# Second mixer: the values of groups 1 and 2 from x itself in fp32, with the norm's weights in the moving operand

## The chip, the cores and the metric

The kernel runs on one core of a Trainium2 chip. The metric is device time in microseconds (us) of one execution, as the median over several runs. TensorE's clock is granted at one of two levels, 1.2 or 2.4 GHz; the profile gives it as a share, 0.5 or 1.0.

## The reference, cut to what matters

A decoder trunk of two layers over 512 tokens, model width 1024. The change is in the second layer's mixer. Each token row of x is normalized, multiplied by a weight per model column, and projected:

```python
def rms_norm(x, g):
    y = x * rsqrt(mean(x * x, axis=-1) + EPS)
    return y * g

proj = rms_norm(x, norm_mix) @ w_in          # 512 x 1024 @ 1024 x 2560
# three groups of four heads, each with q, k, v of 256 columns; (window, dilation):
DIL_PATTERNS = ((128, 1), (512, 4), (2048, 16))
# each query attends to itself and to t-d, t-2d, ... back to t-window
```

The root of a token's mean square is one factor per token, so it may be multiplied in after the projection. The weight g belongs to a model column, which is the dimension that the projection sums over, so it may go to either operand of the product.

## The kernel before, in words

x lies in SBUF transposed (`xT`, 8 blocks of 128 model columns x 512 tokens, fp32). A plain fp32 product is avoided: `prep(3)` makes two tensors from xT times g, `xh` (rounded to the type fp32r) and `xl` (the rest), and each weight tile is split by `wsplit` into `wh` and `wl` in the same way. A product is then the three fp32r matmuls xh wh, xl wh and xh wl.

`layer1` is woven from two generators. `products` issues the projections: two tiles for the memory heads' queries, four tiles of queries and keys of group 0, the values of group 0, tiles 6 to 9 of the groups 1 and 2 (first pair of heads), the values of group 1, tiles 10 to 13 (second pair of heads), the values of group 2, then the output projection's memory half. `attention` issues memory attention, scores, transposes and the products with the values. `_weave` takes their steps in turn. The order on TensorE is as written; on the other engines and the DMA queue a planner orders the instructions by a simulated time line.

`values(g)` computes the values of group g with tokens on the partitions: the stationary operand is a block of 128 tokens of xh or xl, the moving one 256 columns of the weights (line 403 to 405 in `token_major`). Group 0 takes neighbouring tokens. Groups 1 and 2 take tokens by their residue modulo 4, so every fourth column is read (`by_residue`). Per group there are 4 blocks of tokens and 8 blocks of model columns. Line 1010 multiplies the result by the factor per token on ScalarE and puts it into `v`.

Weights are loaded on SP's DMA queue into `wf`, a ring of two buffers of one megabyte (`load`, line 168; a load waits until the buffer's last reader is done). `wh` and `wl` are rings of three. `token_weights(..., True)` splits the value weights in two halves: the first with cast and subtraction on VectorE (lines 50, 51), the second with the cast on ScalarE (line 48) and the subtraction on GpSimd. Loads of the second layer go through the two buffers in this order: seven of the input projection (two tiles each) with the three of the values among them, one for each half of the output projection, then those of the feed-forward network.

The strided stationary operand and full fp32 matmuls both occur elsewhere: `ssq_cols` (line 256) sums squares per token with a moving operand of 2 columns of ones, once with neighbouring tokens and once by residue, and the final norm (line 1185) multiplies 128x256 in fp32.

Of the kernel before, what the change touches and what calls it, by code (L numbers as in the profile page):

```python
# [12 lines left out]
AF = mybir.ActivationFunctionType  # L13
ALU = mybir.AluOpType
# [3 lines left out]
KT = D // 128  # L18
# [46 lines left out]
class _Trunk:  # L65
# [328 lines left out]
            wl += [l[:, k * n:(k + 1) * n] for k in range(4)]  # L394
        return wh, wl

    def token_major(self, out, w, ks, xh, xl, i, by_residue=False):

        wh, wl = w
        mm = self.nc.tensor.matmul  # L400
        b = slice(i, None, 4) if by_residue else slice(i * 128, (i + 1) * 128)
        for k in ks:
            mm(out, xh[k][:, b], wh[k], start=k == 0, stop=False)
            mm(out, xl[k][:, b], wh[k], start=False, stop=False)
            mm(out, xh[k][:, b], wl[k], start=False, stop=k == KT - 1)
# [531 lines left out]
    def layer1(self):  # L937
        nc, mm = self.nc, self.nc.tensor.matmul
        xh, xl, parts = self.prep(3)
        ws = self.chunks("in1", list(range(14)), lo=("gpsimd", "vector"), hi=(None, None))  # L940
        pq = []
        for j in range(2):
            p = self.psum_any()
# [41 lines left out]
        def g12_scores(pr, r, QK):  # L985
# [6 lines left out]
            for s in range(2):  # L992
                if r + s == 0:
# [2 lines left out]
                                P[1, pr][:, s * 1024 + r * 256:s * 1024 + (r + 1) * 256],  # L996
                                st12[pr][:, r, s:s + 1], st12[pr][:, r, 2 + s:3 + s])

        def values(g):
            w = self.token_weights(self.io["v1"][g], 256, True)  # L1000
            for r in range(4):
                p = self.psum("acc")[:, :256]
                for k in range(0, KT, 4):
                    self.token_major(p, w, range(k, k + 4), xh, xl, r, by_residue=g > 0)
                    if k == 0:
                        yield
                if r == 0:
                    V[g] = self.big("v", F32)
                c = cols if g == 0 else self.cols4
                self.values(p, c[:, r:r + 1], V[g][:, r * 256:(r + 1) * 256])  # L1010
                yield
# [56 lines left out]
        def products():  # L1068
# [3 lines left out]
            done.add("qk0")  # L1072
            yield from qk(0, qk0[1])
            yield from values(0)
            done.add("qk1")
            done.add("v0")
# [3 lines left out]
            for n, _ in enumerate(values(1)):  # L1080
                if n == 4:
                    done.add("qk2")
                yield
# [5 lines left out]
            for n, _ in enumerate(values(2)):  # L1089
                if n == 0:  # L1090
                    mem_out = [(o, self.inverse(den)) for o, den in self.mem_out]
                if n == 4:
                    done.add("qk3")
                if n == 4:
                    mem_out = [self.finish_pair(*a) for a in mem_out]
                yield
# [241 lines left out]
```

## Time and profile before

| | before |
|---|---|
| median of 3 runs | 1280.42 us (1276.65 to 1281.71) |
| profiled execution | 1287.35 us, span 1285.6 us |
| mean granted clock | 0.973 |
| TensorE matmul | 1218.7 us (95% of the span) |
| TensorE weight load | 983.7 us (77%) |
| VectorE | 586.0 us (46%) |
| ScalarE | 498.7 us (39%) |
| GpSimd | 389.4 us (30%) |
| DMA | 109.98 MB, 86 GB/s |

The engines are PE (TensorE's matmuls), PEld (its weight loads, which overlap them), DVE (VectorE), ACT (ScalarE), POOL (GpSimd) and SP (the queue that issues the loads). Matmuls are pipelined: the durations shown contain the drain and overlap, so the pace of a sequence is read from the starts. Times are from the start of the span.

### The profile page before, as it was taken

What the parts mean: (1) busy time and instruction counts of PE and PEld (TensorE: products, weight loads), DVE (VectorE), ACT (ScalarE), POOL (GpSimd) and SP (SyncE); (2) the same over time, 40 slices, a digit from 0 to 9 for tenths busy, and PEclk for the clock granted to TensorE, in tenths of its full rate; (3) what the DMA queues carried; (4) which work ended last, traced back from release to release, by engine and by line L of the source; (5) the groups of instructions that cost most, each with busy time, mean ns of one, the idle gap of its engine ahead of it and who ended that gap; (6) DMA issues with size and microseconds to landing.
All of it is one profiled execution on the core that took longest, in us unless ns stands there. A gap on an engine that the chain in (4) does not pass through costs nothing.

```text
span 1285.6 us, 14958 instructions
## 1 busy us (share of the span) xinstructions
PE 1218.7 (95%) x5868; PEld 983.7 (77%) x5868; DVE 586.0 (46%) x1054; ACT 498.7 (39%) x859; POOL 389.4 (30%) x242
## 2 busy tenths in 40 slices
PE   6688979999999999999998999999999999999997
PEld 5467657677888888888886779887788888888886
DVE  7789976548333333322224542548533333331212
ACT  6564666525323322322223764534332233222222
POOL 4637464244222122212222322333322221121222
PEclk9789999999999999999998999989899999999998
DMA  5402132212222222222233111211222222222221
GB/s 179 131 33 101 49 113 72 70 36 97 78 88 97 98 99 98 78 90 90 90 111 107 66 66 34 97 35 41 92 98 89 80 94 98 99 90 90 91 90 66
DMA packets 30214, 109.98 MB, mean 86 GB/s; under 512 B 2495, under 2 KB 12095, under 8 KB 21695
## 3 DMA queue, kind: packets, MB, share of 16 engines
q1 hardware_dynamic: 29598, 108.50, 24.1%
q8 instruction: 46, 0.75, 0.2%
q10 hardware_dynamic: 544, 0.52, 0.1%
q14 instruction: 26, 0.20, 0.0%
HBM read 105.74 MB, written 3.28 MB: 85 GB/s over the span
## 4 chain that ended last, share of the span: by engine, by line
PE 81%; DVE 12%; DMA 3%; issue 1%; ACT 1%; POOL 1%; SPq 0%; DVEq 0%; ACTq 0%; POOLq 0%
PE psS L226 5%; PE psS L225 5%; PE psS L227 5%; PE psT L225 3%; PE psT L227 3%; PE psT L226 3%; PE psacc L225 3%; PE psacc L226 3%; PE psacc L227 3%; PE psacc L200 3%; PE psS L414 3%; PE psS L200 3%; PE psS L202 3%; PE psS L201 3%; PE psacc L202 3%; PE psacc L201 3%
## 5 line engine op out<-in xcount | busy, mean ns | idle before, releaser
L51 POOL TENSOR_TENSOR wl<-wf,wh 128x1024 fp32r<-128x1024 f32 x98 | 238.5, 2434 | 684.6 <-ACT wh L48 621.8
L48 ACT CAST wh<-wf 128x1024 fp32r<-128x1024 f32 (+1 forms) x178 | 183.6, 1032 | 527.9 <-issue 171.3
L51 DVE TENSOR_TENSOR wl<-wf,wh 128x1024 fp32r<-128x1024 f32 (+1 forms) x95 | 118.5, 1247 | 94.1 <-ACT wh L48 94.1
L225 PE MATMUL psS<-xh,wh 128*128 128x512 f32 x296 | 120.0, 405 | 6.8 <-ACT wh L48 6.8
L227 PE MATMUL psS<-xh,wl 128*128 128x512 f32 x296 | 119.2, 403 | 2.8 <-DVE wl L51 2.8
L226 PE MATMUL psS<-xl,wh 128*128 128x512 f32 x296 | 118.9, 402 | 2.8 <-DVE xl L310 2.8
L225 PE MATMUL psT<-xh,wh 128*128 128x512 f32 x200 | 81.1, 405 | 0.0
L227 PE MATMUL psT<-xh,wl 128*128 128x512 f32 x200 | 80.7, 403 | 0.0
L226 PE MATMUL psT<-xl,wh 128*128 128x512 f32 x200 | 80.7, 403 | 0.0
L225 PE MATMUL psacc<-xh,wh 128*128 128x512 f32 x192 | 77.3, 403 | 0.0
L226 PE MATMUL psacc<-xl,wh 128*128 128x512 f32 x192 | 76.9, 401 | 0.0
L227 PE MATMUL psacc<-xh,wl 128*128 128x512 f32 x192 | 76.9, 400 | 0.0
L225 PEld LDWEIGHTS psS<-xh,wh 128*128 128x128 f32 x296 | 56.8, 192 | 20.5 <-ACT wh L48 6.8
L227 PEld LDWEIGHTS psS<-xh,wl 128*128 128x128 f32 x296 | 56.7, 191 | 17.2 <-DVE wl L51 4.2
L226 PEld LDWEIGHTS psS<-xl,wh 128*128 128x128 f32 x296 | 56.8, 192 | 16.7 <-DVE xl L310 3.3
L294 POOL TENSOR_TENSOR ssq<-ssq,t 128x512 f32<-128x512 f32 (+1 forms) x34 | 50.8, 1493 | 55.1 <-ACT t L284 53.9
L213 PE MATMUL psacc<-xh,wh 128*128 128x512 f32 x144 | 62.9, 437 | 0.0
L652 DVE TENSOR_TENSOR raw<-psacc,R 128x512 f32<-128x512 f32 x22 | 15.2, 691 | 103.1 <-PE psacc L227 103.1
L215 PE MATMUL psacc<-xh,wl 128*128 128x512 f32 x144 | 58.1, 404 | 0.0
L214 PE MATMUL psacc<-xl,wh 128*128 128x512 f32 x144 | 58.0, 403 | 0.0
L339 POOL TENSOR_TENSOR raw<-raw,table 128x512 f32<-128x512 f32 x21 | 26.9, 1283 | 72.7 <-ACT raw L336 54.9
L627 DVE TENSOR_TENSOR xT<-xT,psacc 128x512 f32<-128x512 f32 x44 | 30.1, 686 | 38.7 <-PE psacc L202 38.6
(335 smaller groups left out, 2812.7 us busy)
## 6 DMA issues: line engine op xcount, KB each, us to landing
wf<-in_gu SPq DMA_DIRECT2D x44, 1024.0 KB
wf<-in_dn SPq DMA_DIRECT2D x16, 1024.0 KB
wf<-in_in SPq DMA_DIRECT2D x13, 1024.0 KB
wf<-in_dn SPq DMA_DIRECT2D x16, 384.0 KB
wf<-in_v SPq DMA_DIRECT2D x3, 1024.0 KB
xT<-in_x SPq DMA_DIRECT2D x8, 256.0 KB
wf<-in_mk SPq DMA_DIRECT2D x2, 1024.0 KB
wf<-in_mv SPq DMA_DIRECT2D x2, 1024.0 KB
```

Of the source, the lines that this page charges most:

```text
L48: nc.scalar.copy(hi, src)
L51: lo_engine.tensor_tensor(out=lo, in0=src, in1=hi.bitcast(F32), op=ALU.subtract)
L200: mm(out, wh[k], xh[k], start=first and k == 0, stop=False)
L201: mm(out, wh[k], xl[k], start=False, stop=False)
L202: mm(out, wl[k], xh[k], start=False, stop=last and k == n - 1)
L213: mm(out, wh[:, s], xh[k], start=k == 0, stop=False)
L214: mm(out, wh[:, s], xl[k], start=False, stop=False)
L215: mm(out, wl[:, s], xh[k], start=False, stop=k == KT - 1)
L225: mm(out, wh[:, s], xh[k], start=k == 0, stop=False)
L226: mm(out, wh[:, s], xl[k], start=False, stop=False)
L227: mm(out, wl[:, s], xh[k], start=False, stop=k == KT - 1)
L294: engine.tensor_tensor(out=parts[part], in0=parts[part], in1=sq, op=ALU.add)
```

## The change

The values of groups 1 and 2 no longer use xh, xl, wh and wl. The weights are loaded, and each of their 8 blocks of 256 columns is multiplied in place by g (odd blocks on VectorE, even ones on ScalarE). The matmul then takes xT itself, every fourth column, as stationary operand and the scaled weights as moving operand, both fp32: one matmul in the code per block in place of three. Group 0 keeps its form, and `token_major` loses its flag. Steps of the weave stay where they were.

```diff
--- before.py
+++ after.py
@@ -394,11 +394,11 @@
             wl += [l[:, k * n:(k + 1) * n] for k in range(4)]
         return wh, wl
 
-    def token_major(self, out, w, ks, xh, xl, i, by_residue=False):
+    def token_major(self, out, w, ks, xh, xl, i):
 
         wh, wl = w
         mm = self.nc.tensor.matmul
-        b = slice(i, None, 4) if by_residue else slice(i * 128, (i + 1) * 128)
+        b = slice(i * 128, (i + 1) * 128)
         for k in ks:
             mm(out, xh[k][:, b], wh[k], start=k == 0, stop=False)
             mm(out, xl[k][:, b], wh[k], start=False, stop=False)
@@ -996,12 +996,27 @@
                                 P[1, pr][:, s * 1024 + r * 256:s * 1024 + (r + 1) * 256],
                                 st12[pr][:, r, s:s + 1], st12[pr][:, r, 2 + s:3 + s])
 
+        def scaled_weights(g):
+
+            w = self.load(self.io["v1"][g], [KT * 256])
+            for k in range(KT):
+                b = w[:, k * 256:(k + 1) * 256]
+                if k % 2:
+                    nc.vector.tensor_scalar(b, b, self.gains[:, 3, k:k + 1], None, op0=ALU.mult)
+                else:
+                    nc.scalar.activation(b, b, AF.Copy, scale=self.gains[:, 3, k:k + 1])
+            return w
+
         def values(g):
-            w = self.token_weights(self.io["v1"][g], 256, True)
+            w = scaled_weights(g) if g else self.token_weights(self.io["v1"][g], 256, True)
             for r in range(4):
                 p = self.psum("acc")[:, :256]
                 for k in range(0, KT, 4):
-                    self.token_major(p, w, range(k, k + 4), xh, xl, r, by_residue=g > 0)
+                    if g:
+                        for a in range(k, k + 4):
+                            mm(p, self.xT[:, a, r::4], w[:, a * 256:(a + 1) * 256], start=a == 0, stop=a == KT - 1)
+                    else:
+                        self.token_major(p, w, range(k, k + 4), xh, xl, r)
                     if k == 0:
                         yield
                 if r == 0:
```

## Rows read from the trace of the kernel before

**Rows 1.** The page: busy time of the engines, and the chain that ended last.
```profile
PE 1218.7 (95%) x5868; PEld 983.7 (77%) x5868; DVE 586.0 (46%) x1054; ACT 498.7 (39%) x859; POOL 389.4 (30%) x242
...
PE 81%; DVE 12%; DMA 3%; issue 1%; ACT 1%; POOL 1%; SPq 0%; DVEq 0%; ACTq 0%; POOLq 0%
```

**Rows 2.** Stretches: us; PE, PEld, DVE, ACT, POOL busy; PEclk, DMA share, GB/s.
```profile
779.40:808.20 28.80, 28.80 (x166) 27.29 (x164) 6.39 (x17) 10.67 (x21) 3.65 (x2) 1.00 0.05 13
833.00:862.90 29.90, 28.46 (x154) 27.16 (x153) 12.58 (x24) 11.76 (x26) 8.94 (x7) 0.89 0.12 37
851.20:858.00 6.80, 6.80 (x35) 6.46 (x34) 2.30 (x8) 2.84 (x10) 0.00 (x0) 0.50 0.00 0
```

**Rows 3.** Timeline of PE in group 1's values: start us, duration us, what.
```profile
787.61 0.40 PE L404 MATMUL psacc<-wh,xl 128*128 128x256 f32 x1
...
795.61 0.40 PE L405 MATMUL psacc<-wl,xh 128*128 128x256 f32 x1
```

**Rows 4.** Timeline of PE in group 0's values, neighbouring tokens.
```profile
729.38 0.28 PE L404 MATMUL psacc<-wh,xl 128*128 128x256 f32 x1
...
731.88 0.28 PE L405 MATMUL psacc<-wl,xh 128*128 128x256 f32 x1
```

**Rows 5.** Timeline of PE's weight loads, neighbouring tokens, then by residue.
```profile
680.99 1.10 PEld L256 LDWEIGHTS psacc<-ones,ssq 128*128 128x128 f32 x8
...
688.71 1.50 PEld L256 LDWEIGHTS psacc<-ones,ssq 128*128 128x128 f32 x6
```

**Rows 6.** Line 256, these loads: ns min/median/max, first and last start us.
```profile
L256 PEld LDWEIGHTS psacc<-ones,ssq x8: 188/192/193, 681.0 to 681.9; 128*128 128x128 f32 x8
...
L256 PEld LDWEIGHTS psacc<-ones,ssq x6: 329/329/329, 688.7 to 689.9; 128*128 128x128 f32 x6
```

**Rows 7.** Timeline of PE in the final norm, full fp32.
```profile
1269.31 0.59 PE L1185 MATMUL psacc<-raw,ones 128*128 128x256 f32 x2
```

**Rows 8.** Line 1185: ns min/median/max, first and last start us.
```profile
L1185 PE MATMUL psacc<-raw,ones x4: 377/430/519, 1269.3 to 1277.8; 128*128 128x256 f32 x4
```

**Rows 9.** Timeline of PE, products of 512 columns, neighbouring stationary columns.
```profile
684.20 0.39 PE L225 MATMUL psS<-xh,wh 128*128 128x512 f32 x1
...
686.48 0.39 PE L226 MATMUL psS<-xl,wh 128*128 128x512 f32 x1
```

**Rows 10.** The tile wf: ns min/median/max of its casts, subtractions, scalings.
```profile
L48 ACT CAST wh<-wf x178: 833/1052/1077, 5.7 to 1257.7; 128x1024 fp32r<-128x1024 f32 x162, 128x768 fp32r<-128x768 f32 x16
L51 POOL TENSOR_TENSOR wl<-wf,wh x98: 2348/2403/4253, 21.1 to 1254.8; 128x1024 fp32r<-128x1024 f32 x98
...
L483 DVE TENSOR_SCALAR mh<-wf,gains x4: 343/344/1176, 181.7 to 183.3; 128x256 fp32r<-128x256 f32 x4
L485 ACT ACTIVATE mh<-wf,gains x4: 499/506/522, 181.8 to 183.0; 128x256 fp32r<-128x256 f32 x4
```

**Rows 11.** Timeline of SP's queue: loads of tiles 12, 13 and out1b.
```profile
774.34 0.37 SPq L176 DMA_DIRECT2D wf<-in_in  x1
...
831.30 0.37 SPq L176 DMA_DIRECT2D wf<-in_out1b  x1
```

**Rows 12.** Stretches, the DMA behind the load of 774.34.
```profile
775.30:778.80 3.50, 3.50 (x24) 2.30 (x24) 1.77 (x2) 1.72 (x2) 0.26 (x1) 1.00 0.89 300
```

**Rows 13.** Timeline of PE, the first product of tile 12.
```profile
822.00 0.39 PE L213 MATMUL psacc<-xh,wh 128*128 128x512 f32 x1
```

**Rows 14.** Timeline of PE and ACT in group 2; [idle before <-releaser].
```profile
847.52 0.59 ACT L443 COPY frow<-psT 128x512 f32<-128x512 f32 x1 [2.76 <-PE psT L427]
...
849.17 0.33 PE L414 MATMUL psS<-qkh 64*128 64x128 f32 x2 [0.77 <-ACT qkh L48]
...
850.29 0.33 PE L414 MATMUL psS<-qkl,qkh 64*128 64x128 f32 x2 [0.68 <-DVE qkl L51]
```

**Rows 15.** Timeline of PE in group 2's values, at half clock.
```profile
855.78 0.44 PE L405 MATMUL psacc<-wl,xh 128*128 128x256 f32 x1
...
857.88 0.37 PE L405 MATMUL psacc<-wl,xh 128*128 128x256 f32 x1
```

## The prediction

> **What bounds the kernel now.** I read the page first: TensorE is busy 95% of the span and carries 81% of the chain of waits, so a change in its work counts unless something else is late where it is made [rows 1]. Then the table of stretches, cut at the two places that the change touches. The values of group 1 lie in 779.4 to 808.2 us, those of group 2 in 833.0 to 862.9 [rows 2]. In the first stretch TensorE is busy all of its 28.80 us at full clock, VectorE 6.39, ScalarE 10.67, GpSimd 3.65: nothing beside it is near its limit. In the second it is busy 28.46 of 29.90, and 6.8 us of it run at half clock. So the time of these products is what the stage costs, almost one for one.
>
> What a product costs is read from starts in the timeline, since the listed durations contain the drain and overlap. In group 1, 34 products of 256 columns start between 787.61 and 795.61: 8.00/34 = 0.2353 us each [rows 3]. Group 0 does the same three products per block with a stationary block of neighbouring columns: 22 starts from 729.38 to 731.88, 0.1136 us each [rows 4]. The moving operand is the same width, so the doubled time belongs to the load of a stationary block taken at every fourth column.
>
> The row sums show that the load alone does it. The small products that sum squares (2 columns, fp32) show loads back to back with nothing to stream: 8 neighbouring ones take 1.10 us, and with 0.19 for the last, (1.10-0.19)/7 = 0.13 each; 6 strided ones take 1.50, one of them 0.329 long, (1.50-0.33)/5 = 0.234 each [rows 5, 6]. That is the 0.2353 of group 1 to within 1%.
>
> **The change part by part.** *The products.* Each of groups 1 and 2 has 4 residues x 8 blocks x 3 = 96 products now. They take 96 x 0.2353 = 22.6 us. Afterwards there are 4 x 8 = 32 matmuls in full fp32. The trace shows how such a matmul runs: the small sums are 4 matmuls in the code and 8 loads and 8 products in the trace, so each is two load-and-product pairs [rows 5, 6]. Hence 64 pairs per group, each with a strided load. What the load of a strided fp32 block costs is in the same rows: 0.234. What two passes over 256 fp32 columns cost is in the final norm: a matmul of 128x256 whose two products span 0.59 us, one being 0.377 long, so 0.59-0.377 = 0.21 from start to start [rows 7, 8].
>
> Not shown is a strided fp32 load together with a 256-column fp32 product. From below, the pair can't be shorter than its load, 0.234; from above, load and product one after the other are 0.234+0.21 = 0.446. I take 0.236, next to the lower end, for two reasons: the strided load with a 256-column single pass costs 0.2353, hardly more than the load alone, so that product lies beneath the load; and 512-column products with their loads start every (686.48-684.20)/10 = 0.228 us, where load and columns in turn would be 0.13 plus at least 0.21 [rows 9]. Then a group takes 64 x 0.236 = 15.1 us in place of 22.6, and the two groups save 2 x 7.5 = **15.0 us**. With 0.25 for the pair it would be 2 x (22.6-16.0) = 13.2. The break-even lies at 22.6/64 = 0.353.
>
> The Trainium skill speaks against this in "TensorE: Matmul & The Clock Gate", "Part 3: Packing small matmuls — row/col tiling": a weight load overlaps with a running matmul only when the row groups differ, which full 128-row blocks never do. By that rule the sum is the 0.446 and the change is a loss (first rival); the 0.228 and the 0.2353 above disagree with it. The same page's "LDWEIGHTS (loading the stationary operand)" prices a load by its columns alone, 128/1.2 = 107 ns; an estimate from it, with no dearer load for strides, puts the old form at group 0's 96 x 0.1136 = 10.9 us and the new one at 64 x 0.21 = 13.4, a loss of 2.5 per group. The strided rows at 0.234 disagree with it and decide.
>
> *Preparing the weights.* Removed per group: a cast and a subtraction on VectorE, a cast of 1.05 us on ScalarE, a subtraction of 2.40 on GpSimd. Added: 4 scalings of 128x256 on ScalarE at 0.51 (2.0 us) and 4 on VectorE at 0.34 (1.4) [rows 10]. TensorE waits for them only if they come late. Group 1's weights were cast and freed by 774.34, when the next load took their buffer [rows 11], 5 us before they are used; the scalings need less time and don't wait for buffers of the split halves. I count nothing. If the cover were gone, 2.0 us per group would show.
>
> *The buffer held longer.* The weights now are the moving operand, so one of the two load buffers is held until the group's last product. The load of tiles 12 and 13 of the input projection, issued at 774.34, then waits until group 1 ends, by 808.2-7.5 = 800.7. On the SP queue group 2's weights, then the output projection's, stand behind it. A megabyte lands 4.5 us after its issue: the DMA is busy until 778.8 for the load of 774.34 [rows 11, 12]. So tiles 12 and 13 are in at 805.2; cast and subtraction add 1.05+2.40, 808.7. TensorE starts on tile 12 at 822.0 now [rows 13], 814.5 then: 5.8 us to spare. Group 2's weights land behind them, about 809.7 if the two share the queues, and are wanted at 833.0-7.5 = 825.5. The second output projection's load waits for group 2's end, about 862.9-15.0 = 848, where it went at 831.3; its product comes after the attention's last join, so I count nothing there. If the 5.8 were used up, TensorE would wait in front of tile 12 for what is missing.
>
> *Split buffers set free.* Tiles 10 to 13 no longer queue for the three split buffers behind the values. That takes work off the moment when the values end; TensorE was not waiting for it, so nothing.
>
> *The wait in group 2.* TensorE stands at 849.17 and 850.29 for 0.77+0.68 us, because the last query/key cast sits on ScalarE behind a copy that waits for TensorE's own transposes; the clock falls behind it [rows 2, 14]. After the change TensorE arrives there 40 x 0.236 = 9.4 us after tile 13, not 14. If the cast goes ahead of the copy the wait goes, up to 1.5 us gained; if the order stays, so does the wait, and the clock matters more. At half clock the old products still start every (857.88-855.78)/9 = 0.233 us [rows 15], since the load sets their pace; the new ones would need twice 0.21 = 0.42 there. A stretch of 6.8 us would pass 16 of them, not 29: 13 x 0.236 = 3.1 us lost. From -3.1 to +1.5, I take 0.
>
> **The sum.** The profiled execution took 1287.35 us, 1285.6 of it span and 1.75 around it; minus 15.0 it would be 1272.3. It lies 6.9 above the median of the runs, 1280.42. The saving is TensorE's own time in two stretches at full clock for the most part, so I take it off the median: **1265.4 us**.
>
> **The rivals.**
> 1. *Load and product in turn.* Place: the 128 pairs of the two groups; price 0.446 each, so 2 x (28.5-22.6) = 11.8 us more, 1292. It decides from 0.353 per pair on. For it: no row has this pair. Against: [rows 3, 9].
> 2. *New waits and half clock eat it.* Shorter values cover less of ScalarE's and VectorE's chain (their order is planned anew), and each wait brings a half-clock stretch that now costs. One such wait as at 849 in each group: 2 x (1.5+3.1) = 9.2 lost, 1280.4-15.0+9.2 = 1274.6. For it: the wait at 849 exists. Against: the first stretch has none, with ScalarE busy 10.7 of 28.8. A late tile 12 belongs here.
> 3. *Another engine sets the end.* If the attention's chain through ScalarE and VectorE needed the whole stretch anyway, nothing is gained: 1280. Against: their busy time [rows 2].
>
> **How the numbers follow.** The forecast 0.78, its own range 1262 to 1270 (a pair at 0.25 and some wait above; the wait at 849 gone below). Rival 2 0.12, rival 1 0.06, rival 3 0.04. A measurement of this kernel can tell some 0.5% from no change, 6.4 us: faster means below 1274.0. The forecast and over half of rival 2 lie there: 0.86. Same, with the rest of rival 2 and rival 3: 0.08. Slower: 0.06. Range 1261 to 1275: it takes in the pair's cost up to 0.28 and most of rival 2, and leaves out the serial end.
>
> **What the profile after would show.** 64 products per group starting every 0.236 us, the loads 0.33 long; the stretch of group 1 about 21.3 us, that of group 2 about 22.4. The load of tiles 12 and 13 issued as group 1 ends and no idle time of TensorE ahead of tile 12. The wait in group 2 gone or as before. The prediction is wrong if the pairs start more than 0.30 us apart, if TensorE idles over 5 us more between 779 and the feed-forward, or if the products fall into a half-clock stretch for over 10 us.

## The result and the profile after

The changed kernel takes 1266.37 us (median of four runs) where the kernel before, beside it on the same chip, takes 1280.45: a ratio of 0.9882 [0.9844, 0.992]. One of the four runs was slow, 2760 us; the ratio leaves it out, and the median of the other three is 1265.67. Three more timings gave 0.9916 [0.9887, 0.9944], 0.9901 [0.9874, 0.9927] and 0.9885 [0.9854, 0.9916]. The forecast was 1265.4. The profiled execution took 1261.48 us, 1259.8 of it span.

Two lines of the page of the changed kernel: busy time, share of the span and instructions of the engines, the answer to [rows 1].

```profile
PE 1191.5 (95%) x5804; PEld 963.8 (77%) x5804; DVE 585.3 (46%) x1058; ACT 499.7 (40%) x865; POOL 385.7 (31%) x240
...
PE 78%; DVE 13%; DMA 3%; ACT 2%; POOL 2%; issue 2%; SPq 0%; DVEq 0%; POOLq 0%; ACTq 0%
```

TensorE has 64 products fewer (192 became 128) and 27.2 us less busy time, nearly twice what the change is worth by the timings. So the page alone does not answer how large the gain is. The stretches of the values of groups 1 and 2 do (columns as in [rows 2]):

```profile
773.00:794.80 21.80, 21.80 (x135) 19.70 (x132) 5.20 (x16) 10.27 (x24) 3.62 (x2) 1.00 0.00 1
819.50:842.40 22.90, 20.54 (x122) 19.03 (x121) 10.58 (x23) 12.65 (x27) 6.06 (x5) 1.00 0.14 47
```

Group 1 went from 28.80 us to 21.80, group 2 from 29.90 to 22.90. Group 2 now holds 2.36 us in which TensorE is idle, and no half clock. From the first product of group 1 to the first of the output projection that follows both groups, the changed kernel shows these starts in TensorE's timeline:

```profile
773.06 2.13 PE L1017 MATMUL psacc<-wf,xT 128*128 128x256 f32 x8
...
842.31 0.49 PE L200 MATMUL psacc<-oh,wh 128*128 128x512 f32 x1
```

That is 69.25 us. The same two starts of the kernel before lie at 779.44 and 862.84, 83.40 apart. **The stage is 14.15 us shorter.** Added up from each product's start to the next instruction's start: group 1's products 23.62 to 16.44 (-7.2), group 2's 23.08 to 16.20 (-6.9); the old wait of [rows 14] is gone (-1.45); a new one came (+2.36); attention scores that had run at half clock run at full (-0.65). Together -13.8, which leaves 0.3 to small things.

The two spans differ by 25.8 us, not 14. About 9.4 of the rest lie in the feed-forward stages, which no edit touches: the two stretches of the code from the first feed-forward to layer 1, and from the last one's start to the end, took 368.97 and 362.49 us in the profile before and 364.34 and 357.71 in this one (counted from the product of line 268 in each, the first to that of layer 1, the second to the end of the last product). Two rows, first before, then after, of the same length of time within the first feed-forward:

```profile
320.00:520.00 200.00, 200.00 (x859) 162.01 (x858) 69.05 (x91) 59.71 (x74) 43.25 (x18) 1.00 0.25 90
```
```profile
320.00:520.00 200.00, 200.00 (x875) 163.97 (x874) 70.96 (x94) 61.78 (x77) 43.30 (x18) 1.00 0.26 95
```

TensorE is never idle and the granted clock is 1.00 in both, yet one runs 859 products and the other 875: products of 512 columns start 0.2333 us apart in one execution and 0.2289 in another. Either pace comes in either stage, whatever the edit: the repeated profile of the changed kernel has 368.97 in the first and 357.7 in the last, the run below with fp32 and neighbouring columns has the slower pace in the last alone, and edited forms of the kernel before have the faster one in both. So a comparison of two profiles is made here on the stage that was changed, and of kernels on the timings.

### The profile page after: what moved, and what is told of

The parts are those of the page before. It is cut to its first block, busy times and chain, and to the rows that moved or that the text cites. A ratio compares the mean times of both kernels' runs of the same rounds, so it can differ in the third digit from the quotient of the medians.

```text
span 1259.8 us, 14831 instructions
## 1 busy us (share of the span) xinstructions
PE 1191.5 (95%) x5804; PEld 963.8 (77%) x5804; DVE 585.3 (46%) x1058; ACT 499.7 (40%) x865; POOL 385.7 (31%) x240
## 4 chain that ended last, share of the span: by engine, by line
PE 78%; DVE 13%; DMA 3%; ACT 2%; POOL 2%; issue 2%; SPq 0%; DVEq 0%; POOLq 0%; ACTq 0%
PE psS L227 5%; PE psS L226 5%; PE psS L225 5%; PE psT L226 3%; PE psT L227 3%; PE psT L225 3%; PE psacc L227 3%; PE psacc L226 3%; PE psacc L225 3%; PE psacc L200 3%; PE psS L200 3%; PE psS L202 3%; PE psS L201 3%; PE psS L414 3%; PE psacc L202 3%; PE psacc L201 3%
## 5 line engine op out<-in xcount | busy, mean ns | idle before, releaser
L51 POOL TENSOR_TENSOR wl<-wf,wh 128x1024 fp32r<-128x1024 f32 x96 | 233.7, 2436 | 636.3 <-ACT wh L48 594.0
L48 ACT CAST wh<-wf 128x1024 fp32r<-128x1024 f32 x176 | 181.2, 1031 | 512.8 <-issue 164.2
```

Source lines behind the costliest of these rows:

```text
L48: nc.scalar.copy(hi, src)
L51: lo_engine.tensor_tensor(out=lo, in0=src, in1=hi.bitcast(F32), op=ALU.subtract)
```

## The experiments

Theory L: the pace of a pair is set by the load of a block taken at every fourth column, and the gain is the number of such loads. Theory P: the gain comes from the work that left the other engines (casts, split buffers). Theory W: waits and the clock decide, not the products. The times of stages below are differences of starts in the timelines. In all of them the ratio is to the kernel before on the same chip.

**The changed kernel again.** No edit.

> The changed kernel once more, beside the next three. Theory L (the strided load sets the pace: 64 loads at 0.233 us per group in place of 96): the pairs start 0.233 apart, the stretch of group 1's values takes 21.8 us, that of group 2 22.9 with a wait of 2.4 us in it, and the run 1265 to 1268. Theory P (the gain comes from the splits that are gone and the buffers they freed, not from TensorE) and theory W (it comes from the wait and the half-clock stretch in group 2 that are gone) expect the same of this run.

1266.44 us, 0.9916 [0.9887, 0.9944]; the stage is 69.27, the new wait is there. The later two, with no edit either:

> The changed kernel once more, beside the three above: 1264 to 1268, with the wait of 2.4 us in group 2.

> The changed kernel beside it: 1264 to 1268, one wait of 2.4 us in group 2.

1265.81 and 1261.84 us; the last lies below the 1264 to 1268 expected.

**Three passes, neighbouring columns** (the kernel before, edited):

```
-        b = slice(i, None, 4) if by_residue else slice(i * 128, (i + 1) * 128)
+        b = slice(i * 128, (i + 1) * 128)
```

> The kernel before, with groups 1 and 2 reading neighbouring tokens as stationary operand (the values stand in other places, so the output is another). Theory L: the products start 0.114 us apart, not 0.235; 96 x 0.114 = 10.9 us per group in place of 22.6, 23 us less in all, from which waits for the query/key chain take back up to 3.5 per group: 1257 to 1264. Theories P and W: the splits, the buffers and the order of the other engines are those of before, so 1280 (P), or no less than 1278 (W).

1258.34 us, 0.9861 [0.9831, 0.9891]. One of the three passes, by its loads (ns, minimum/median/maximum):

```profile
L403 PEld LDWEIGHTS psacc<-wh,xh x64: 186/188/330, 774.1 to 837.1; 128*128 128x128 f32 x64
```

The products start 0.114 to 0.118 apart, and group 1 takes 12.1 us instead of 23.6, with all casts and splits in place. That is the price of the stride by itself: 11.5 us of products in a group, more than the 7.2 of the change. P and W cannot give this.

**Full fp32, neighbouring columns** (the changed kernel, edited):

```
-  mm(p, self.xT[:, a, r::4], w[:, a * 256:(a + 1) * 256], start=a == 0, stop=a == KT - 1)
+  mm(p, self.xT[:, a, r * 128:(r + 1) * 128], w[:, a * 256:(a + 1) * 256], start=a == 0, stop=a == KT - 1)
```

> The changed kernel, with neighbouring tokens in place of every fourth (another output). Theory L: the load falls to 0.13 and the columns set the pace, 0.213 to 0.215 per pair, 64 x 0.215 = 13.8 in place of 15.0: 1.2 us less per group, 1263 to 1265, and the stretch of group 1 20.6. If the fp32 products themselves set the 0.233, the pace stays and so does the time, 1266. Should load and product still add up partly, the pace falls by more than 0.02.

1263.37 us, 0.989 [0.9858, 0.9923]. Its timeline in group 1, and the loads of both groups:

```profile
781.64 4.70 PE L1017 MATMUL psacc<-wf,xT 128*128 128x256 f32 x21
```
```profile
L1017 PEld LDWEIGHTS psacc<-wf,xT x128: 186/190/337, 775.2 to 841.9; 128*128 128x128 f32 x128
```

With 0.379 for the last, (4.70-0.379)/20 = 0.216 per pair. With a cheap load the two passes over 256 fp32 columns set the pace; with a strided one, at 0.233, the load does. The columns of the changed kernel lie almost wholly beneath its loads. In this run a half-clock stretch fell on the values of group 2, the granted clock being the seventh figure of the stretch's row:

```profile
826.90:830.30 3.40, 3.40 (x10) 2.68 (x9) 0.69 (x1) 0.00 (x0) 2.66 (x2) 0.50 0.00 0
```

Pairs start 0.427 apart there, twice 0.21, while the loads beneath them have time to spare.

**Two passes of three, strided** (the kernel before, the xl product left out in groups 1 and 2):

```
-            mm(out, xl[k][:, b], wh[k], start=False, stop=False)
+            if not by_residue:
+                mm(out, xl[k][:, b], wh[k], start=False, stop=False)
```

> The kernel before, with the product of the low part of x left out in groups 1 and 2: 64 fp32r products per group, each with a strided load, splits and buffers as before. Theory L: 64 loads at 0.234 = 15.0 us per group whatever the columns (one pass here, two in the changed kernel), so the same stretch of 21.8 to 22 us for group 1 as the changed kernel, and 1265 to 1268. Theory P: nothing of the preparation is saved, 1280. Theory W: as the wait in group 2 falls, 1276 to 1280.

1266.32 us, 0.9929 [0.9898, 0.996]. 64 strided loads as in the changed kernel, but one-pass products, splits and old buffers. Its loads:

```profile
L403 PEld LDWEIGHTS psacc<-wh,xh x64: 307/330/335, 772.3 to 841.7; 128*128 128x128 f32 x64
```

The products start 0.235 apart and group 1 takes 16.12 us, against 16.44 in the changed kernel. The number of strided loads decides, whether one pass or two are streamed over them. Two parts of group 2's stretch ran at half clock in this run:

```profile
824.10:827.50 3.40, 3.40 (x16) 3.40 (x16) 0.69 (x1) 0.00 (x0) 2.03 (x3) 0.50 0.00 0
834.30:842.50 8.20, 8.20 (x46) 7.29 (x45) 3.31 (x12) 3.66 (x12) 2.36 (x1) 0.50 0.01 2
```

Its products kept starting 0.233 apart there, and the group took 17.53 us including a wait of 1.5: load-bound products hardly feel the clock, as [rows 15] had shown.

**The splits kept** (the changed kernel, with an unread split of each half of the weights, cast and subtraction, ahead of the scaling):

```
+            for c in range(2):
+                self.wsplit(w[:, c * 1024:(c + 1) * 1024], (nc.vector, nc.gpsimd)[c], (nc.vector, None)[c])
```

> The changed kernel, which also does the old casts and subtractions of the value weights of groups 1 and 2 ahead of the scaling, into halves that nothing reads. Theory L (the gain is the 64 strided loads in place of 96): TensorE's stretches stay as in the changed kernel, 21.8 and some 23 us, and the run 1264 to 1269. Theory P (the gain is the splits that are gone): back to 1275 to 1280.

1262.52 us, 0.9873 [0.9847, 0.9898]. Its stretches of the two groups:

```profile
773.80:795.60 21.80, 21.80 (x134) 19.69 (x132) 9.14 (x18) 12.14 (x26) 3.69 (x3) 1.00 0.12 48
822.50:844.30 21.80, 21.77 (x121) 19.96 (x121) 11.77 (x24) 12.54 (x28) 8.73 (x6) 0.92 0.14 49
```

VectorE is busy 9.14 us instead of 5.20 in group 1's stretch, ScalarE 12.14 instead of 10.27, and TensorE's time stays 21.80. The stage is 70.35 us (69.25 without the splits); the 1.1 lie in group 2, part of which ran at half clock here (0.92), and the run came out a little below the 1264 expected. P's casts and subtractions fall: work taken from engines that were not late is worth nothing here. No product holds the split halves in this run; that holding them is not the price either is shown by the run of two passes, which holds them and gains as much in group 1.

**Every second column** (the kernel before, blocks of tokens at a stride of 2):

```
-        b = slice(i, None, 4) if by_residue else slice(i * 128, (i + 1) * 128)
+        b = slice(i // 2 * 256 + i % 2, i // 2 * 256 + 256, 2) if by_residue else slice(i * 128, (i + 1) * 128)
```

> The kernel before (three passes), with every second token of 256 in groups 1 and 2 as stationary operand, not every fourth (another output). A stride of four fp32 is 16 bytes, two are 8. If only a stride of 16 bytes or more is dear, the products start some 0.114 to 0.13 us apart and the run is that of neighbouring tokens, 1257 to 1262. If any stride is, they stay 0.235 apart and the run 1278 to 1282. If the price goes with the bytes skipped, it lies between, near 0.17, and the run near 1268. The Trainium skill (SBUF — State Buffer, the part on cachelines) has lines of 16 bytes with full bandwidth for at least two hits per line; that speaks for the first.

1261.05 us, 0.9864 [0.9835, 0.9893]. Its loads, and two starts of its products in group 1, 20 products apart:

```profile
L403 PEld LDWEIGHTS psacc<-wh,xh x64: 193/195/331, 772.7 to 839.4; 128*128 128x128 f32 x64
```
```profile
779.72 0.28 PE L403 MATMUL psacc<-wh,xh 128*128 128x256 f32 x1
...
782.12 0.28 PE L405 MATMUL psacc<-wl,xh 128*128 128x256 f32 x1
```

2.40/20 = 0.120. A stride of two fp32 columns (8 bytes) costs 0.120 against 0.114 for neighbours; a stride of four (16 bytes) costs 0.235. The price is not linear in the stride: it lies between these two.

**Where the new wait comes from.** In group 2 of the changed kernel the second block of values waits. Its timeline of TensorE, VectorE and ScalarE (in brackets the idle time before, and what ended it):

```profile
819.51 3.88 PE L1017 MATMUL psacc<-wf,xT 128*128 128x256 f32 x16
...
822.20 1.14 ACT L48 CAST qkh<-raw 128x512 fp32r<-128x512 f32 x1 [1.76 <-DVE raw L340]
823.36 2.34 ACT L336 COPY raw<-psacc 32x512 f32<-32x512 f32 x4
825.75 3.64 PE L1017 MATMUL psacc<-wf,xT 128*128 128x256 f32 x14 [2.36 <-ACT raw L336]
```

The accumulators named psacc have two banks. The bank wanted holds tile 13's projection until ScalarE has copied it; ScalarE first casts the result of the tile before it, for which it waits 1.76 us itself, and ends its copies at 825.70. The block of values between takes 16 x 0.233 = 3.7 us now, where it took 24 x 0.234 = 5.6 and covered those copies: before, they ended 0.3 us ahead of need. The kernel of three passes over neighbouring columns, whose blocks are short too and which has all the splits, shows the same wait:

```profile
PE psacc L403 <- ACT raw L336: 2.4, 1, 2.4
```

So it comes with a shorter block, whatever shortens it. Another bank for that one block, in the changed kernel:

```
-                p = self.psum("acc")[:, :256]
+                p = self.psum("O" if g == 2 and r == 1 else "acc")[:, :256]
```

> The changed kernel, with the second block of group 2's values accumulated in the bank of tag O, which nothing uses then. If the wait of 2.4 us in group 2 is for the bank that the last query/key projection holds until ScalarE has copied it, it goes: the stretch of group 2 falls from 22.9 to 20.5, and the run by 2.4 us, 1262 to 1265. If the wait comes with the order on ScalarE and moves on, to the third block's bank or to the last keys, the stretch falls by less than 1 us.

1263.21 us, 0.9868 [0.9842, 0.9894]. What TensorE waited for in the edited kernel, layer 1's attention (us in total, times, longest):

```profile
PE psO L385 <- DVE pt L419: 1.5, 1, 1.5
PE psS L414 <- ACT qkh L48: 0.7, 1, 0.7
PE psS L414 <- DVE qkl L51: 0.7, 1, 0.7
```

The wait for L336 is gone and the two of [rows 14] are back, 1.4 us. The stage is 68.29: 1.0 less, not 2.4. In the changed kernel the new wait had covered the old ones. With the scores that need the last keys put later as well:

```
-                if n == 4:
+                if n == 6:
```

> The changed kernel with the second block of group 2's values in the bank of tag O, and the last scores released two steps of the values later (n == 6, not 4), so that both waits on the last query/key chain are covered by products: the two that the other bank alone left (0.7 + 0.7 us) go as well. From the start of group 2's values to the first product of the output projection 0.5 to 1.5 us less than with the other bank alone, if the scores then don't hold up the attention's end; the run 1261 to 1264. If the attention's chain after the scores (softmax, transposes, the products with the values) sets the end, what is gained in group 2 shows up as waits between there and the feed-forward, and the run stays at 1263 to 1266.

```profile
PE psO L226 <- DVE xl L310: 2.8, 1, 2.8
PE psT L427 <- DVE pt L419: 0.8, 1, 0.8
PE psacc L200 <- DVE xT L627: 0.8, 2, 0.5
PE psT L427 <- ACT f L443: 0.3, 1, 0.3
```

None of these waits lies in group 2's values. The stage is 64.37, 3.9 less than with the other bank alone where 0.5 to 1.5 was expected; but 24 of the 48 score products that lay in it now come after its end, so it can't be compared. Taken on to line 268 in the feed-forward, so that all 48 lie in it again, it is 116.81, against 119.8 with the other bank alone and 120.7 to 122.3 in the four profiles of the changed kernel. The timing, 1263.82 us, 0.9877 [0.9843, 0.9911], does not tell it from the change. So the profile shows 3.9 to 5.5 us, part of it from a half-clock stretch that was shorter than in three of those four (3.4 us, not 6.8); that they are a gain in time is not shown.

**Residues two apart for every block** (the changed kernel with the forms exchanged: groups 1 and 2 in three passes again, their xh and xl stored in pairs so that a residue's tokens stand 8 bytes apart; group 0 in full fp32 from xT. The lines that store the pairs):

```
+            if pairs:
+                h, l = (a.rearrange("p (h n q) -> p n h q", h=2, q=2) for a in (h, l))
+                x = x.rearrange("p (n h q) -> p n h q", h=2, q=2)
```

> The same output in another way: xh and xl of the second mixer are stored so that tokens of one residue modulo 4 stand two apart, not four (pairs of tokens 4n, 4n+1 in one half, 4n+2, 4n+3 in the other); groups 1 and 2 keep three passes, group 0 takes fp32 products of x with scaled weights, neighbouring tokens. If the dear load goes with a stride of 16 bytes, as every second token showed: the products of groups 1 and 2 start 0.12 apart, 11.6 us per group in place of 15.0, group 0 64 x 0.216 = 13.8 in place of 11: about 4 us less than the changed kernel, 1259 to 1263. The price is that the projections' moving operand is read in pairs of tokens. If that costs, the 512-column products of the second mixer start over 0.24 apart; at 0.45, 14 tiles x 24 x 0.22 = 74 us are lost, 1335.

> As the one before, and the second block of group 2's values in the bank of tag O: the wait for the query/key projection's bank, 2.4 us, goes, the one for the last keys of 1.4 stays or grows by what is no longer waited before. 1 to 2.4 us less than the one before, 1257 to 1262.

1284.17 us, 1.0042 [1.0025, 1.0059], and with the other bank 1289.41, 1.0081 [1.0054, 1.0107]. Both times were missed: the first expectation had named the price that came, but as a condition; the second missed as a whole. The values do start 0.121 apart and group 0's pairs 0.216, as expected. But the same xh and xl are the moving operand of the input projection, and are read there in pairs. Two starts in its timeline, 4 products apart:

```profile
765.48 0.50 PE L214 MATMUL psacc<-xl,wh 128*128 128x512 f32 x1
...
766.79 0.50 PE L215 MATMUL psacc<-xh,wl 128*128 128x512 f32 x1
```

1.31/4 = 0.327 us for 512 columns, where contiguous ones take 0.229. Counted from each start to the next instruction's, the products of lines 213 to 215 take 100.5 us, against 76.4 in the changed kernel: the values' gain is paid back there, several times over.

## Why the prediction was right

*Products.* Forecast 64 pairs at 0.236 us per group, 15.0 us for both. In the changed kernel's timeline and loads (ns):

```profile
779.76 4.60 PE L1017 MATMUL psacc<-wf,xT 128*128 128x256 f32 x19
```
```profile
L1017 PEld LDWEIGHTS psacc<-wf,xT x128: 307/329/330, 773.0 to 840.9; 128*128 128x128 f32 x128
```

With 0.397 for the last, (4.60-0.397)/18 = 0.2335. The lower bound was the right one: the product lies beneath the load. The first pair of a block behind other work takes 0.44, the first product 0.35 before, so a group gained 7.2 and 6.9, not 7.5. The first rival, 0.446 a pair, is refuted by every block. The Trainium skill's "TensorE: Matmul & The Clock Gate", "Part 3: Packing small matmuls — row/col tiling", by which only loads to other row groups overlap a running matmul, does not hold for these full blocks: 0.233 with the load, 0.216 where the load is cheap. One reading was off: the 0.13 of a neighbouring load takes in the gap before the second load. The later ones of [rows 5] start 0.112 apart; no term of the sum used it.

*Preparing the weights.* Counted as nothing, and it was: the changed kernel's tile wf shows (ns, first and last start)

```profile
L1005 DVE TENSOR_SCALAR wf<-wf,gains x8: 345/348/354, 746.2 to 800.0; 128x256 f32<-128x256 f32 x8
L1007 ACT ACTIVATE wf<-wf,gains x8: 492/496/512, 746.2 to 800.3; 128x256 f32<-128x256 f32 x8
```

Group 2's scalings end 19 us before its first product, and the prices are those of [rows 10].

*The buffer held longer.* The total was right, the step was not. SP's queue in the changed kernel:

```profile
767.09 0.37 SPq L176 DMA_DIRECT2D wf<-in_in  x1
...
794.05 0.34 SPq L176 DMA_DIRECT2D wf<-in_v  x1
805.27 0.37 SPq L176 DMA_DIRECT2D wf<-in_out1a  x1
...
818.74 0.37 SPq L176 DMA_DIRECT2D wf<-in_out1b  x1
...
841.59 0.34 SPq L176 DMA_DIRECT2D wf<-in_gu  x1
```

The load of tiles 12 and 13 took the other buffer, at 767.09, before group 1 had begun. That buffer held tiles 10 and 11, and its last reader was this subtraction, first in the kernel before, then in the changed one:

```profile
804.55 1.23 DVE L51 TENSOR_TENSOR wl<-wf,wh 128x1024 fp32r<-128x1024 f32 x1 [3.08 <-ACT wh L48]
```
```profile
765.80 1.21 DVE L51 TENSOR_TENSOR wl<-wf,wh 128x1024 fp32r<-128x1024 f32 x1
```

It starts 25 us after group 1's first product in the one, 7 us before it in the other. That fits the split buffers set free, which the prediction had counted as nothing; no run tests it by itself. It was group 2's weights that waited for group 1's last product, and the feed-forward's first ones for group 2's. Neither made TensorE wait. I had followed the right rule (a moving operand holds its buffer to the end) with the wrong buffer. Taken in turn, group 1's would have been next; the two were not used in turn, and which one a load takes has to be read from what released it.

*The wait in group 2.* Between 3.1 us lost and 1.5 gained, taken as 0. Measured: 1.45 gained from the old wait, 2.36 lost to one that I had not named, in front of a bank and not of a cast. The cast did go ahead of the copy, but that is not what ended the old wait. With the other bank it goes ahead too, and the wait is back:

```profile
831.42 1.09 ACT L48 CAST qkh<-raw 128x512 fp32r<-128x512 f32 x1 [2.25 <-DVE raw L340]
832.42 0.58 ACT L443 COPY frow<-psT 128x512 f32<-128x512 f32 x1
```

In the changed kernel the new wait covers the old one. The new one is the kind of rival 2 (a shorter value block covers less of ScalarE's chain), at one place of the two, without its half clock. I had listed SBUF buffers and no accumulator banks. With the scores that came back to full clock (0.65 gained) the net is 0.3 lost: near the 0 by offsets, which is luck and not foresight.

*At half clock* the pairs were put at 0.42; the run with neighbouring columns shows 0.427. In the changed kernel's profile none fell there.

*Rival 3*, another engine setting the end, is out: e.g. with the splits kept group 1's stretch stayed at 21.80. *The sum*: 15.0 forecast for the stage, 14.15 measured there; by the medians 14.1 here, and 11.3, 12.4 and 16.2 in the repeats. The forecast was set on the median and not on the profiled execution (1287.35-15.0 = 1272.3), and that mattered: that execution had the slower pace in both feed-forward stages.

## What to carry over

Before cutting passes, read what a product costs against its load alone: here the load of a strided block was the price, so that a full fp32 matmul with fewer loads was faster, and the layout cost more than the passes. Where a product that hides other work is shortened, list each ring that feeds it, accumulator banks too, and ask how near its last release was to need: 0.3 us of slack was used up. And compare profiles by stage: untouched stages can differ by more than half of what the change brings.

## What was not expected of the hardware

One-pass products of 256 columns, each over a load of 128 stationary columns, start 0.114 to 0.12 us apart at a stride of 1 or 2 fp32 values, and 0.233 at a stride of 4. The Trainium skill's "SBUF — State Buffer" says in "Door 1: The DMA port swizzle" that memory has lines of 16 bytes, and that full bandwidth takes at least two accesses to a line; the step between stride 2 and stride 4 agrees with that, though no run here shows the lines themselves. The same note counts a stride of 4 fp32 values as still free; the 0.233 decides against it. A moving operand has a price for its layout too: read in pairs of 8 bytes it takes 0.327 us per 512 columns, not 0.229. No run reads a stationary and a moving operand in the same way, so which of them feels it more is not shown. And the same products of 512 columns run at 0.2289 or 0.2333 us apart with a granted clock of 1.00 in both; what sets the one or the other stays open.
